# One decoder layer on one core: plain fp32 products, rotation tables on VectorE, and idle ticks in the state-space pipeline

## Chip, cores and metric

The kernel runs on 1 core of one Trainium2 chip. The metric is the device time of one execution in microseconds (us). Runs of a few executions each give a median, and one further execution is taken apart by the hardware profiler.

## What is computed

The reference is one decoder layer that mixes a state-space model (SSM) with sliding-window attention, for a prompt of 2048 tokens and for 8 single sample tokens with stored state, all in fp32. The part that the change touches is the SSM: 64 groups of 16 channels, each with a complex state of 64 numbers.

```python
def ssm_segment(u, hr, hi, ar, ai, bbr, bbi, c_re, c_im):
    xr = jnp.einsum('btgc,gpc->btgp', u, bbr)
    xi = jnp.einsum('btgc,gpc->btgp', u, bbi)
    ...
    _, _, sr, si = lax.associative_scan(
        complex_combine, (jnp.broadcast_to(ar, shp), jnp.broadcast_to(ai, shp), xr, xi), axis=1)
    y = (jnp.einsum('btgp,gcp->btgc', sr, c_re.astype(jnp.float32))
         - jnp.einsum('btgp,gcp->btgc', si, c_im.astype(jnp.float32)))
    return y, sr[:, -1], si[:, -1]
```

Around it stand the projection of the modulated input by `w_in`, the attention, a gated product with `w_glu`, two branch products, the product with `w_out` and a layer norm.

## The kernel before

All large products (line 78, in `chunk_k`) run on TensorE (PE) with operands of type float32r. Each fp32 operand is split into hi and lo, hi on ScalarE (ACT) and the rest on VectorE (DVE), and three products are summed. A job is one block of 128 weight columns against five chunks of tokens (512, 512, 512, 256 and 264), each over 8 slices of 128 features, so 8 x 3 products a chunk.

The program runs in phases. Phase 1 makes the first projections and the SSM's parameters (`ssm_prep`), which are packed into one table a group, `packD`. **Phase 2** (`phase2`) runs 20 jobs of the projection with the SSM woven in: after slices 2, 5 and 7 of every chunk one *tick* of the SSM pipeline is issued, so there are 300 ticks. Phase 3 weaves the attention into more jobs, phases 4 and 5 do the rest.

The SSM works on 32 pairs of groups (`ssm_pairs`). `pipeline` starts a new pair every 9 ticks and gives a pair one stage a tick:

- `load`: the pair's parameters `pk` and inputs `u` come in by DMA, issued by SyncE (SP).
- `b_mat`: DVE makes `bt` in five operations (lines 722 and 724). `rot_tables` makes the rotation tables of the first group.
- `c_mat`: PE transposes `bt` (L752), ACT and DVE split the result `bl` and ACT and GpSimd (POOL) split `u`. DVE makes `ce` in five operations (L759, L761), then come the second group's rotation tables.
- `t_mat`: PE multiplies `pk` by `ce` (L771), ACT copies the result to `kt` (L776), DVE adds a diagonal (L779), SP writes `kt` to DRAM (`tD`) and reads it back shifted as `tt` (L785).
- `x_in`: PE makes `xp` from `bl` and `u`; ACT and DVE split `tt` and `ce`; DVE rotates `xp` into the rotating frame (L798 to L803).
- `scan`: two scans on DVE (L808), four operations that rotate back into `S` (L814 to L817), and a split of `S`.
- an empty stage, then `y_out`: PE makes `yp` from `tt`, `u`, `ce`, `S`; ACT applies gelu (L829), SP stores.

`rot_tables` runs on POOL (lines 744 to 746): six operations of 128 x 256 a group, twelve a pair. The helper `passes` (L703) does three float32r products for one fp32 product, the helper `split` does a copy on ACT (L696) and a subtraction (L697):

```python
for i, (a, b) in enumerate(((wh, xh), (wh, xl), (wl, xh))):
    nc.tensor.matmul(ps, a[:, g], b[:, g, xs], start=first and i == 0, stop=last and i == 2)
```

The scratch tile of `rot_tables` and the tile `kt` share one buffer (tag `tm`, one copy). Each engine executes its own queue in order. That order is set when the program is built, by a scheduler that goes by the priority of the program order and by its own estimate of when operands are ready; so instructions of one pair stand between those of its neighbours.

Of the kernel before, what the change touches and what calls it, by code (L numbers as in the profile page):

```python
# [19 lines left out]
T = 2048  # L20
# [3 lines left out]
G = 64  # L24
# [4 lines left out]
PK = 180  # L29
oBB, oBBs, oW, oWs, oPR, oPI, oRR, oRI, oC1, oS1, oC2, oS2, oR8, oHO, oAH = 0, 16, 32, 48, 64, 73, 82, 90, 98, 114, 130, 146, 162, 164, 172  # L30
# [9 lines left out]
class Trunk:  # L40
# [8 lines left out]
    def split_w(self, parts, st=None):  # L49
        """parts: (dram AP [n, ...], tile slice function)"""  # L50
# [29 lines left out]
    def products(self, jobs, X, nxt=None, tick=None, first=ORD):  # L80
        """jobs: (weight parts, evac(c, ps), begin, end); the next weights are split while a job runs"""
# [26 lines left out]
    def phase_in(self):  # L108
# [32 lines left out]
        with ExitStack() as pes:  # L141
# [36 lines left out]
            def ada(k):  # L178
                """shift and 1 + scale of features 128 k .., by feature"""
# [118 lines left out]
    def ssm_prep(self):  # L298
# [4 lines left out]
        def small(name):  # L303
            return p.tile([128, G], F32, name=name)

        def signed(name, t):
            s = small(name)
# [60 lines left out]
        crs, cis = signed("crs", cr), signed("cis", ci)  # L368
# [6 lines left out]
        for i in range(3):  # L375
            n = (small(f"ec{i}"), small(f"es{i}"))
            self._cmul(v, n, e, e, t1, t2)
            e = n
        e8 = e
        for i in range(4):  # L380
            tg = (f"ec{i % 2}", f"es{i % 2}") if i < 3 else ("fc", "fs")
            n = (small(tg[0]), small(tg[1]))
# [14 lines left out]
        # sample state: h_old and a * h_old  # L397
# [41 lines left out]
        for qd in range(4):  # L439
# [36 lines left out]
            # e^{i n th8}: n = 1..16, and n = 0, 16, .., 240  # L476
            for oC, oS, e, first in ((oC1, oS1, e8, 1), (oC2, oS2, e128, 0)):
# [29 lines left out]
                v.tensor_scalar(pk[0:64, :, oS:oS + 16], pk[0:64, :, oS:oS + 16], -1.0, None, op0=OP.mult)  # L507
                yield
# [162 lines left out]
    def pipeline(units, stages, ii):  # L671
        """at tick t every unit u runs stage t - ii * u, older units first"""
# [9 lines left out]
    def ssm_pairs(self, p, pp, ii):  # L682
# [10 lines left out]
        def split(name, x, eng, bufs=1):  # L693
            hi = p.tile(list(x.shape), F32R, name=name + "h", bufs=bufs)
            lo = p.tile(list(x.shape), F32R, name=name + "l", bufs=bufs)
            nc.scalar.copy(hi, x)  # L696
            eng.tensor_tensor(lo, x, hi, op=OP.subtract)  # L697
            return hi, lo

        def passes(ps, w, x, g, xs, first, last):  # L700
            (wh, wl), (xh, xl) = w, x
            for i, (a, b) in enumerate(((wh, xh), (wh, xl), (wl, xh))):
                nc.tensor.matmul(ps, a[:, g], b[:, g, xs], start=first and i == 0, stop=last and i == 2)  # L703

        def load(s):
# [6 lines left out]
            s["u"] = p.tile([128, 2, 272], F32, name="u", bufs=1)  # L712
# [14 lines left out]
        def rot_tables(s, g):  # L727
            pk = s["pk"]
            if g == 0:
                s["cs"] = p.tile([128, 2, 256], F32, name="cs")  # L730
                s["sn"] = p.tile([128, 2, 256], F32, name="sn")
            tm = p.tile([128, 256], F32, name="tm", bufs=1)
            tv = tm.rearrange("p (a b) -> p a b", a=16)
# [71 lines left out]
        def scan(s):  # L805
# [14 lines left out]
            s["S"] = split("S", S[:, :, 0:264], v)  # L820
# [585 lines left out]
```

## Time and profile before

| what | value |
| --- | --- |
| median of 3 runs | 2398.24 us (2396.42 to 2400.52) |
| span of the profiled execution | 2395.4 us |
| PE busy | 2284.5 us (95%) |
| DVE busy | 1479.4 us (62%) |
| ACT busy | 810.6 us (34%) |
| POOL busy | 678.4 us (28%) |
| DMA, mean over the span | 132 GB/s |

Of the profiled execution the span from the first to the last instruction is what is recorded; the median of the runs is 2.8 us above it. "Busy" counts the time in which an engine has at least one instruction in work; for PE the ends of the products are modelled, so a short stall can hide in it. The share of an engine over the whole span is an average over phases: in the 40 slices of the profile page DVE is at 8 or 9 tenths in slices 7 to 15 (360 to 900 us), at 1 to 2 tenths just before, and lower after.

### The profile page before, as it was taken

The numbers are of one execution on the slowest core, as the hardware profiler recorded it, in microseconds if no ns is written. First come the engines' busy times: TensorE is split into PE (matmuls) and PEld (weight loads), VectorE is DVE, ScalarE is ACT, GpSimd is POOL, SyncE is SP. The second block draws the span as 40 slices with busy tenths as digits, with TensorE's granted clock in tenths as the row PEclk, the third lists the DMA queues.
The fourth block names the chain that finished last, engine by engine and source line by source line (L and its number), as shares of the span: only waits on it lengthen the run. The fifth ranks groups of instructions, "written<-read, shape, count | busy, mean of one in ns | idle before, by whom it ended". The sixth has DMA issues, their size and how long they took to land. (4 is left out here: it accounts for less than half of the span.)

```text
span 2395.4 us, 36160 instructions
## 1 busy us (share of the span) xinstructions
PE 2284.5 (95%) x13011; PEld 1916.6 (80%) x13011; DVE 1479.4 (62%) x3032; ACT 810.6 (34%) x1764; POOL 678.4 (28%) x828
## 2 busy tenths in 40 slices
PE   7999998999999999899999999999999999999998
PEld 5888886777778778777878888887877888888886
DVE  4895129998999996137786666516435214223887
ACT  3411113333222222136675655536223213212100
POOL 1100027666777764000100000012443000222232
PEclk9999999999999999899999999999999999999999
DMA  9453623333343343733334333257535646767431
GB/s 284 101 149 126 197 66 104 102 102 105 99 110 103 104 110 91 143 113 115 101 111 137 103 95 113 82 139 174 153 102 179 199 123 184 218 196 219 156 117 69
DMA packets 388755, 317.03 MB, mean 132 GB/s; under 512 B 90582, under 2 KB 332654, under 8 KB 386991
## 3 DMA queue, kind: packets, MB, share of 16 engines
q1 hardware_dynamic: 388576, 314.73, 45.9%
q8 instruction: 102, 1.67, 0.3%
q14 instruction: 77, 0.63, 0.1%
HBM read 194.75 MB, written 122.11 MB: 132 GB/s over the span
## 5 line engine op out<-in xcount | busy, mean ns | idle before, releaser
L78 PE MATMUL acc<-hh,whi 128*128 128x512 f32 (+2 forms) x2000 | 705.7, 353 | 11.3 <-ACT zr L580 10.5
L78 PE MATMUL acc<-hl,whi 128*128 128x512 f32 (+2 forms) x2000 | 703.9, 352 | 0.0
L78 PE MATMUL acc<-hh,wlo 128*128 128x512 f32 (+2 forms) x2000 | 701.8, 351 | 0.0
L78 PEld LDWEIGHTS acc<-hh,whi 128*128 128x128 f32 x2000 | 379.5, 190 | 63.0 <-ACT zr L580 10.9
L78 PEld LDWEIGHTS acc<-hh,wlo 128*128 128x128 f32 x2000 | 379.8, 190 | 51.8 <-issue 6.7
L78 PEld LDWEIGHTS acc<-hl,whi 128*128 128x128 f32 x2000 | 380.4, 190 | 50.2 <-issue 7.2
L78 PE MATMUL acc<-xh,whi 128*128 128x512 f32 (+2 forms) x960 | 337.3, 352 | 16.6 <-ACT sg L1200 13.9
L78 PE MATMUL acc<-xl,whi 128*128 128x512 f32 (+2 forms) x960 | 336.4, 350 | 1.3 <-DVE xl L1148 1.2
L78 PE MATMUL acc<-xh,wlo 128*128 128x512 f32 (+2 forms) x960 | 335.1, 349 | 0.0
L78 PEld LDWEIGHTS acc<-xh,whi 128*128 128x128 f32 x960 | 182.7, 190 | 44.2 <-ACT sg L1200 17.4
L78 PEld LDWEIGHTS acc<-xl,whi 128*128 128x128 f32 x960 | 182.7, 190 | 26.0 <-DVE xl L1148 3.4
L1078 POOL TENSOR_TENSOR o<-o,z 128x512 f32<-128x512 f32 x32 | 42.6, 1330 | 565.7 <-ACT o L1077 517.7
L78 PEld LDWEIGHTS acc<-xh,wlo 128*128 128x128 f32 x960 | 182.3, 190 | 23.1
L1148 DVE TENSOR_TENSOR xl<-xst,xh 128x1024 fp32r<-128x1024 f32 (+2 forms) x84 | 104.8, 1265 | 78.1 <-ACT xh L1147 77.0
L59 DVE TENSOR_TENSOR wlo<-wst,whi 128x1024 fp32r<-128x1024 f32 x74 | 97.5, 1318 | 86.4 <-ACT whi L58 85.6
L1045 DVE SCALAR_TENSOR_TENSOR t<-ps,bias 128x512 f32<-128x512 f32 (+1 forms) x128 | 82.6, 670 | 98.6 <-PE ps L1043 96.3
L882 ACT ACTIVATE t<-t,nm 128x256 f32<-128x256 f32 (+1 forms) x256 | 125.5, 493 | 46.0 <-DVE es L879 29.9
L1235 POOL TENSOR_TENSOR sg<-sg,zs 128x512 f32<-128x512 f32 (+2 forms) x40 | 48.7, 1219 | 314.0 <-DMA xst<-ysD 190.5
L745 POOL TENSOR_TENSOR tm<-pk 128x256 f32<-128x256 f32 x128 | 106.8, 834 | 65.2 <-DMA tD<-kt 59.0
L1147 ACT CAST xh<-xst 128x1024 fp32r<-128x1024 f32 (+2 forms) x84 | 86.0, 1044 | 102.2 <-DMA xst<-mD 33.9
L58 ACT CAST whi<-wst 128x1024 fp32r<-128x1024 f32 x74 | 77.6, 1049 | 102.9 <-PE acc L78 95.1
L580 ACT COPY zr<-acc 128x512 f32<-128x512 f32 (+2 forms) x120 | 59.9, 500 | 137.0 <-PE acc L78 58.1
(372 smaller groups left out, 3935.2 us busy)
## 6 DMA issues: line engine op xcount, KB each, us to landing
wst<-in_w_in SPq DMA_DIRECT2D x50, 512.0 KB
uD<-u SPq DMA_DIRECT2D x8, 1088.0 KB
u<-uD SPq DMA_DIRECT2D x32, 272.0 KB
yD<-y SPq DMA_DIRECT2D x64, 132.0 KB
x<-in_x_prompt SPq DMA_DIRECT2D x16, 512.0 KB
wa<-in_w_ada SPq DMA_DIRECT2D x16, 512.0 KB
qf<-qD SPq DMA_DIRECT2D x32, 256.0 KB
z<-zaP SPq DMA_DIRECT2D x32, 256.0 KB
```

The costliest lines, as they stand in the source:

```text
L58: nc.scalar.copy(hi, st)
L59: nc.vector.tensor_tensor(lo, st, hi, op=OP.subtract)
L78: self.nc.tensor.matmul(ps[:, :n], w[:, k, :], x[:, k, :], start=(k == 0 and i == 0), stop=(k == KT - 1 and i == 2))
L580: nc.scalar.copy(z[:, :n], ps[:, :n])
L745: gq.tensor_tensor(tv, up(x2), lo(y2), op=OP.mult)
L882: nc.scalar.activation(t1[:, h, kw], t1[:, h, kw], AF.Exp, bias=nm[:, h:h + 1], accum_out=den[:, h:h + 1])
L1045: v.scalar_tensor_tensor(t1[:, 2 * g:2 * g + 2, kw], ps[:, :, kw], 0.125, s["bias"][:, hd, b0:b0 + kw.stop], op0=OP.mult, op1=OP.add)
L1078: nc.gpsimd.tensor_tensor(o4, o4, s["z4"], op=OP.mult)
L1147: nc.scalar.copy(xv(hi[:, k - 1:k + 1]), sv(st))
L1148: nc.vector.tensor_tensor(xv(lo[:, k - 1:k + 1]), sv(st), xv(hi[:, k - 1:k + 1]), op=OP.subtract)
L1235: gq.tensor_tensor(t[:, :n], t[:, :n], pa[:, :n], op=OP.add)
```

## The change

- **Products.** The SSM's products take the fp32 operands as they are, one instruction where three stood. The splits of `bl`, `u`, `tt`, `ce` and `S` go, with their ten float32r tiles.
- **Rotation tables.** `rot_tables` moves from POOL to DVE. Cosine and sine of a group stand in one tile and are made by three operations of 128 x 512 instead of six of 128 x 256. This needs a table `-S` of 16 more numbers a group in `packD` (196 instead of 180), made by one more DVE operation for each quarter of the groups in `ssm_prep`.
- **Idle ticks and buffers.** Empty stages are put after `load`, after `x_in` and after `scan`: 12 stages instead of 8, so the last pair ends at tick 291 instead of 287. `u`, `ce`, `tt` and `S` get two buffers instead of one. The tile `tm` is twice as large, still one copy, and still shared with `kt`.
- In `ssm_prep` some small tiles share buffers by tag.

```diff
-PK = 180
+PK = 196
...
             for oC, oS, e, first in ((oC1, oS1, e8, 1), (oC2, oS2, e128, 0)):
...
+                if not first:
+                    v.tensor_scalar(pk[:, :, oN2:oN2 + 16], S, -1.0, None, op0=OP.mult)
...
-            s["u"] = p.tile([128, 2, 272], F32, name="u", bufs=1)
+            s["u"] = p.tile([128, 2, 272], F32, name="u")
...
-            for out, (x1, y1), (x2, y2), op in ((s["cs"], (oC2, oC1), (oS2, oS1), OP.subtract),
-                                                (s["sn"], (oS2, oC1), (oC2, oS1), OP.add)):
-                ov = out[:, g].rearrange("p (a b) -> p a b", a=16)
-                gq.tensor_tensor(ov, up(x1), lo(y1), op=OP.mult)
-                gq.tensor_tensor(tv, up(x2), lo(y2), op=OP.mult)
-                gq.tensor_tensor(ov, ov, tv, op=op)
+            ov = s["rot"][:, :, g].rearrange("p e (a b) -> p e a b", a=16)
+            v.tensor_tensor(ov, up(oC2), lo(oC1), op=OP.mult)
+            v.tensor_tensor(tm.rearrange("p e (a b) -> p e a b", a=16), up(oN2), lo(oS1), op=OP.mult)
+            v.tensor_tensor(s["rot"][:, :, g], s["rot"][:, :, g], tm, op=OP.add)
...
-            s["bl"] = split("bl", ps, v)
-            s["us"] = split("u", s["u"], gq, 2)
-            ce = s["ce"] = p.tile([128, 2, 9, 16], F32, name="ce", bufs=1)
+            s["bl"] = p.tile([128, 2, 128], F32, name="bl", bufs=1)
+            nc.scalar.copy(s["bl"], ps)
+            ce = s["ce"] = p.tile([128, 2, 9, 16], F32, name="ce")
...
-                passes(xp[:, g, :264], s["bl"], s["us"], g, slice(8, 272), True, True)
-            s["tts"] = split("tt", s["tt"], v)
-            s["ces"] = split("ce", s["ce"][:, :, 1:9].rearrange("p g j c -> p g (j c)"), v)
+                nc.tensor.matmul(xp[:, g, :264], s["bl"][:, g], s["u"][:, g, 8:272], start=True, stop=True)
...
-            s["S"] = split("S", S[:, :, 0:264], v)
...
-                passes(yp[:, g, :264], s["tts"], s["us"], g, slice(0, 264), True, False)
-                passes(yp[:, g, :264], s["ces"], s["S"], g, slice(0, 264), False, True)
+                nc.tensor.matmul(yp[:, g, :264], s["tt"][:, g], s["u"][:, g, 0:264], start=True, stop=False)
+                nc.tensor.matmul(yp[:, g, :264], s["ce"][:, g, 1:9].rearrange("p j c -> p (j c)"), s["Sf"][:, g, 0:264],
+                                 start=False, stop=True)
...
-        stages = [load, b_mat, c_mat, t_mat, x_in, scan, lambda s: None, y_out]
+        stages = [load, gap, b_mat, c_mat, t_mat, x_in, gap, scan, gap, gap, gap, y_out]
```

How the built order moves is seen at three places. First DVE, a stretch of phase 2 from the making of `ce` to the scans; before, the subtractions of the splits (L697) stand among them:

```order
L759 TENSOR_TENSOR tmp<-pk 128x144 x2
L697 TENSOR_TENSOR bll<-tr,blh 128x256
L697 TENSOR_TENSOR cel<-ce,ceh 128x256
L759 TENSOR_TENSOR ce<-pk 128x144 x2
L779 TENSOR_TENSOR kt<-dg,tr 16x16 x2
L798 TENSOR_TENSOR t_7336<-xp,cs 128x512
L799 TENSOR_TENSOR S<-xp,sn 64x2x256
L800 TENSOR_TENSOR S<-xp,sn 64x2x256
L802 TENSOR_TENSOR hnew<-pk,xp 128x16
L761 TENSOR_TENSOR ce<-ce,tmp 128x288
L803 TENSOR_TENSOR t_7336<-t_7336,S 128x512
```

and now:

```order
L750 TENSOR_TENSOR ce<-ce,tmp 128x288
L768 TENSOR_TENSOR kt<-dg,tr 16x16 x2
L785 TENSOR_TENSOR t_6819<-xp,rot 128x512
L786 TENSOR_TENSOR S<-xp,rot 64x2x256
L787 TENSOR_TENSOR S<-xp,rot 64x2x256
L789 TENSOR_TENSOR hnew<-pk,xp 128x16
L734 TENSOR_TENSOR tm<-pk 128x512
L790 TENSOR_TENSOR t_6819<-t_6819,S 128x512
L735 TENSOR_TENSOR rot<-rot,tm 128x2x256
L795 SCALAR_TENSOR_TENSOR t_6819<-pk,t_6819 128x256 x2
L734 TENSOR_TENSOR tm<-pk 128x512
```

The splits are gone, the whole of `ce` now stands right ahead of `kt`, and the first write of `tm` by the next pair's table (L734) stands five instructions after `kt` (L768), whose buffer it takes over.

Second PE, the end of a pair's `yp`, its successor's `t_mat` and `xp`; before (L703 is one float32r pass):

```order
L703 MATMUL yp<-Sl,ceh 128x264
L703 MATMUL yp<-Sh,cel 128x264
L771 MATMUL tr<-ce,pk 32x128 x2
L703 MATMUL xp<-uh,blh 128x264
L703 MATMUL xp<-ul,blh 128x264
L703 MATMUL xp<-uh,bll 128x264
L703 MATMUL xp<-uh,blh 128x264
```

and now:

```order
L813 MATMUL yp<-S,ce 128x264
L812 MATMUL yp<-u,tt 128x264
L813 MATMUL yp<-S,ce 128x264
L78 MATMUL acc<-hl_833,whi 128x512
L78 MATMUL acc<-hh_832,wlo 128x512
L760 MATMUL tr<-ce,pk 32x128 x2
L780 MATMUL xp<-u,bl 128x264 x2
```

The order of the pieces is the same; where three or nine passes stood, one or three fp32 products stand. In both orders the products of L78 from the first `xp` to the last are the same in number.

Third SP, the DMA issues of one pair, now (before, the order is the same in kind, with L783, L785, L711 in place of L772, L774, L701):

```order
L701 DMA pk<-packD_77 128x392
L558 DMA qD_95<-kq 128x512
L55 DMA wst<-in_w_in 128x8x128
L703 DMA u<-uD_84 128x2x272
L818 DMA yD_91<-y 8x16x264 x2
L558 DMA qD_95<-kq 128x512
L772 DMA tD_3585<-kt 16x8x128 x2
L774 DMA tt<-tD_3585 128x2x128
```

Loads and stores of a pair wait in one queue with the stores of the projection; none of them moved to another queue.

## Rows read from the trace of the kernel before

**Rows 1.** Busy time by stretch, two stretches of phase 2: PE, PEld, DVE, ACT, POOL.

```profile
core 0: us, PE busy (x) PEld busy (x) DVE busy (x) ACT busy (x) POOL busy (x), PEclk, DMA share, GB/s
340.00:905.00 565.00, 512.16 (x2864) 432.00 (x2864) 522.12 (x867) 172.62 (x336) 393.28 (x555) 0.98 0.37 103
350.00:900.00 550.00, 499.24 (x2796) 421.45 (x2795) 507.74 (x845) 168.78 (x328) 379.62 (x537) 0.98 0.37 105
```

**Rows 2.** One line's instructions (L703): ns min/median/max, first and last start in us.

```profile
L703 PE MATMUL xp<-uh,blh x64: 280/284/587, 345.2 to 929.1; 128*128 128x264 f32 x64
```

**Rows 3.** Groups of PE, 340 to 905 us: count | busy us, mean ns | idle before.

```profile
L703 PE MATMUL yp<-uh,ttl 128*128 128x264 f32 x59 | 19.4, 328 | 10.5 <-DVE ttl L697 10.0
L703 PE MATMUL yp<-Sh,ceh 128*128 128x264 f32 x58 | 19.0, 328 | 16.3 <-ACT Sh L696 15.9
```

**Rows 4.** Waits in 340 to 905 us: us in total, times, longest.

```profile
ACT tth L696 <- DMA tt<-tD: 115.6, 27, 7.1
POOL tm L745 <- DMA tD<-kt: 56.5, 25, 5.0
...
DVE tmp L722 <- DMA pk<-packD: 2.8, 3, 1.0
```

**Rows 5.** Groups of DVE, 340 to 905 us (columns as in rows 3).

```profile
L722 DVE TENSOR_TENSOR tmp<-pk 128x128 f32<-128x128 f32 x62 | 37.4, 636 | 3.0 <-DMA pk<-packD 2.8
...
L817 DVE TENSOR_TENSOR S<-t,S 128x512 f32<-128x512 f32 x30 | 33.3, 1109 | 0.0
...
L798 DVE TENSOR_TENSOR t<-xp,cs 128x512 f32<-128x512 f32 x30 | 20.6, 687 | 6.6 <-PE xp L703 6.1
...
L761 DVE TENSOR_TENSOR ce<-ce,tmp 128x288 f32<-128x288 f32 x31 | 16.0, 517 | 0.1
```

**Rows 6.** DVE instructions by line, whole span (columns as in rows 2).

```profile
L722 DVE TENSOR_TENSOR tmp<-pk x64: 277/709/1446, 337.8 to 904.2; 128x128 f32<-128x128 f32 x64
...
L816 DVE TENSOR_TENSOR t<-t,cs x32: 678/1108/1226, 361.7 to 937.8; 128x512 f32<-128x512 f32 x32
...
L808 DVE TENSOR_TENSOR_SCAN t<-pk,t x64: 658/692/1221, 359.0 to 934.3; 128x256 f32<-128x256 f32 x64
...
L759 DVE TENSOR_TENSOR tmp<-pk x64: 293/307/1471, 340.8 to 910.5; 128x144 f32<-128x144 f32 x64
```

**Rows 7.** Groups of POOL, 340 to 905 us (columns as in rows 3).

```profile
L745 POOL TENSOR_TENSOR tm<-pk 128x256 f32<-128x256 f32 x123 | 102.4, 832 | 62.5 <-DMA tD<-kt 56.5 <-ACT zr L580 1.6
...
L774 POOL TENSOR_TENSOR dg<-ident,dT 16x16 f32<-16x16 f32 x60 | 18.3, 306 | 49.2 <-DVE kt L779 47.0
L819 POOL COPY sfin<-S 128x2 f32<-128x2 f32 x29 | 11.3, 391 | 1.2 <-DVE S L817 1.2
L812 POOL COPY S<-pk 128x16 f32<-128x16 f32 x29 | 8.1, 279 | 11.7 <-DVE Sl L697 10.3 <-DVE kt L779 1.3
```

**Rows 8.** Timeline of PE: start us, duration us; float32r products in a row.

```profile
897.07 0.39 PE L78 MATMUL acc<-hh,whi 128*128 128x512 f32 x1
...
901.15 0.39 PE L78 MATMUL acc<-hh,whi 128*128 128x512 f32 x1
...
908.97 0.28 PE L703 MATMUL yp<-uh,tth 128*128 128x264 f32 x1
...
909.71 0.28 PE L78 MATMUL acc<-hh,wlo 128*128 128x256 f32 x1
```

**Rows 9.** Timeline of PE in phase 3: four plain fp32 products and what follows.

```profile
982.72 1.06 PE L936 MATMUL po<-kts,qm 128*128 128x129 f32 x8
983.61 0.27 PE L930 MATMUL pt<-ident,kc 128*128 128x128 f32 x1
```

**Rows 10.** Timeline of DVE, one pair's `kt` and the operation after `x_in`'s first four.

```profile
616.27 0.35 DVE L779 TENSOR_TENSOR kt<-dg,tr 16x16 f32<-16x16 f32 x2 [1.10 <-ACT kt L776]
...
618.87 1.24 DVE L697 TENSOR_TENSOR cel<-ce,ceh 128x256 fp32r<-128x256 f32 x1
```

**Rows 11.** Timeline of SP, the same pair: the stores of `kt`, then the load that waits for them.

```profile
616.46 0.79 SPq L783 DMA_DIRECT2D tD<-kt  x2
619.24 0.38 SPq L785 DMA_DIRECT2D tt<-tD  x1
```

More of the change, by code (lines that the diff above doesn't have):

```diff
@@ L28 @@
 U0, ZS0, Q0, K0, V0, ZA0, GS0, GA0 = 0, 1024, 2048, 3072, 3328, 3584, 4608, 5632
-PK = 180
-oBB, oBBs, oW, oWs, oPR, oPI, oRR, oRI, oC1, oS1, oC2, oS2, oR8, oHO, oAH = 0, 16, 32, 48, 64, 73, 82, 90, 98, 114, 130, 146, 162, 164, 172
+PK = 196
+oBB, oBBs, oW, oWs, oPR, oPI, oRR, oRI, oC1, oS1, oN2, oC2, oS2, oR8, oHO, oAH = 0, 16, 32, 48, 64, 73, 82, 90, 98, 114, 130, 146, 162, 178, 180, 188
 def _bucket(dist):
@@ L301, in ssm_prep, with small, signed @@
         p, pq, pp = self.prp, self.prp, self.sps
[L303 to L307, printed above, removed]
+        def small(name, tag=None):
+            return p.tile([128, G], F32, name=name, tag=tag or name)
+        def signed(name, t, tag):
+            s = small(name, tag)
             v.tensor_scalar(s[0:64], t[0:64], -1.0, None, op0=OP.mult)
@@ L367, in ssm_prep @@
         v.tensor_tensor(ci, t1, den, op=OP.mult)
-        crs, cis = signed("crs", cr), signed("cis", ci)
+        crs, cis = signed("crs", cr, "dt"), signed("cis", ci, "lr")
         yield
@@ L375, in ssm_prep @@
         for i in range(3):
-            n = (small(f"ec{i}"), small(f"es{i}"))
+            n = (small(f"ec{i}", ("e_x", "hf", "nr")[i]), small(f"es{i}", ("e_r", "th", "den")[i]))
             self._cmul(v, n, e, e, t1, t2)
@@ L380, in ssm_prep @@
         for i in range(4):
-            tg = (f"ec{i % 2}", f"es{i % 2}") if i < 3 else ("fc", "fs")
-            n = (small(tg[0]), small(tg[1]))
+            tg = (("e_x", "e_r"), ("hf", "th"), ("e_x", "e_r"), ("mag", "li"))[i]
+            n = (small(f"fc{i}", tg[0]), small(f"fs{i}", tg[1]))
             self._cmul(v, n, e, e, t1, t2)
@@ L691, in ssm_pairs @@
             nc.sync.dma_start(tD[i][:, 256:368], zt)
[L693 to L703, printed above, removed]
         def load(s):
@@ L729, in rot_tables, with up @@
             if g == 0:
[L730 to L733, printed above, removed]
-            def lo(o):
-                return pk[:, g, None, o:o + 16].to_broadcast([128, 16, 16])
-            def up(o):
-                return pk[:, g, o:o + 16, None].to_broadcast([128, 16, 16])
-            for out, (x1, y1), (x2, y2), op in ((s["cs"], (oC2, oC1), (oS2, oS1), OP.subtract),
-                                                (s["sn"], (oS2, oC1), (oC2, oS1), OP.add)):
-                ov = out[:, g].rearrange("p (a b) -> p a b", a=16)
-                gq.tensor_tensor(ov, up(x1), lo(y1), op=OP.mult)
-                gq.tensor_tensor(tv, up(x2), lo(y2), op=OP.mult)
-                gq.tensor_tensor(ov, ov, tv, op=op)
+                s["rot"] = p.tile([128, 2, 2, 256], F32, name="rot")
+                s["cs"], s["sn"] = s["rot"][:, 0], s["rot"][:, 1]
+            tm = p.tile([128, 2, 256], F32, name="tm", bufs=1)
+            B = [128, 2, 16, 16]
+            def up(o):
+                return pk[:, g, o:o + 32].rearrange("p (e a) -> p e a", e=2)[:, :, :, None].to_broadcast(B)
+            def lo(o):
+                return pk[:, g, None, None, o:o + 16].to_broadcast(B)
+            ov = s["rot"][:, :, g].rearrange("p e (a b) -> p e a b", a=16)
+            v.tensor_tensor(ov, up(oC2), lo(oC1), op=OP.mult)
+            v.tensor_tensor(tm.rearrange("p e (a b) -> p e a b", a=16), up(oN2), lo(oS1), op=OP.mult)
+            v.tensor_tensor(s["rot"][:, :, g], s["rot"][:, :, g], tm, op=OP.add)
         def c_mat(s):
@@ L783, in t_mat @@
                 nc.sync.dma_start(dst, kt[32 * g:32 * g + 16, None].to_broadcast([16, 8, 128]))
-            s["tt"] = p.tile([128, 2, 128], F32, name="tt", bufs=1)
+            s["tt"] = p.tile([128, 2, 128], F32, name="tt")
             nc.sync.dma_start(s["tt"], td[:, :512].rearrange("p (g x) -> p g x", x=256)[:, :, 0:128])
@@ L790, in x_in @@
             for g in range(2):
-                passes(xp[:, g, :264], s["bl"], s["us"], g, slice(8, 272), True, True)
-            s["tts"] = split("tt", s["tt"], v)
-            s["ces"] = split("ce", s["ce"][:, :, 1:9].rearrange("p g j c -> p g (j c)"), v)
+                nc.tensor.matmul(xp[:, g, :264], s["bl"][:, g], s["u"][:, g, 8:272], start=True, stop=True)
             t1 = s["t1"] = p.tile([128, 2, 256], F32, name="t1", bufs=1)
-            s["Sf"] = p.tile([128, 2, 265], F32, name="S", bufs=1)
+            s["Sf"] = p.tile([128, 2, 265], F32, name="S")
             t2 = s["Sf"][:, :, 9:265]
@@ L825, in y_out @@
             for g in range(2):
[L826 to L828 removed]
+                nc.tensor.matmul(yp[:, g, :264], s["tt"][:, g], s["u"][:, g, 0:264], start=True, stop=False)
+                nc.tensor.matmul(yp[:, g, :264], s["ce"][:, g, 1:9].rearrange("p j c -> p (j c)"), s["Sf"][:, g, 0:264],
+                                 start=False, stop=True)
+            y = p.tile([128, 2, 264], F32, name="y", bufs=1)
             nc.scalar.activation(y, yp[:, :, :264], AF.Gelu_apprx_tanh)
@@ L831, in y_out, with gap @@
                 nc.sync.dma_start(self.yD[m][(gl + g) * 16:(gl + g + 1) * 16].rearrange("c j n -> j c n"), y[:, g])
-        stages = [load, b_mat, c_mat, t_mat, x_in, scan, lambda s: None, y_out]
+        def gap(s):
+            pass
+        stages = [load, gap, b_mat, c_mat, t_mat, x_in, gap, scan, gap, gap, gap, y_out]
         return self.pipeline([{"pr": i} for i in range(32)], stages, ii)
```

1 line of the change is left out of this document (removed).

## Prediction

> **What bounds the kernel now.** PE is busy for 95% of the span, so the first idea is that only PE work counts. I looked for the phase in which that is not so. The row of slices has DVE at 8 or 9 tenths from 360 to 900 us, where the SSM is woven into the projection. The table by stretch says it in numbers [rows 1]: from 350 to 900 us DVE is busy for 507.74 of 550 us (92%), POOL for 379.62, and PE for 499.24, so PE has gaps of at least 9%. I then read which work sets the pace. The first `xp` product of the 32 pairs starts at 345.2 us, the last at 929.1 [rows 2]: 584 us for 31 pairs, **18.83 us a pair**.
>
> What PE would need for that is counted from its timeline [rows 8]. From 897.07 to 901.15 us eighteen 512-column float32r products start, one every 0.227 us; from 908.97 to 909.71 six of 264 columns, one every 0.123. (The printed durations, 0.39 and 0.28, overlap; starts are what to read.) Nine ticks are three chunks of 24 products, 72 products; over the five chunk widths their mean is (3 x 0.227 + 2 x 0.123) / 5 = 0.185 us, so 13.3 us. Eighteen SSM passes make 2.2 us, transposes and `t_mat` about 0.5: 16.0 us. PE thus stalls for some 2.8 us a pair. It waits in `yp` for the splits of `tt` and of `S` [rows 3], that is for DVE and ACT. ACT itself stands before the split of `tt`, waiting for a DMA, 115.6 us in all [rows 4]. But DVE, with 92%, has only 18.83 x 0.08 = 1.4 us a pair in which it does not work, so it is the engine to follow.
>
> Part of that work is waiting in disguise. The same operation takes very different times: 277 ns at least and 709 in the median for 128 elements, 678 and 1108 for 512 [rows 6]. Those that read PSUM do not stretch: L798 has a mean of 687 ns [rows 5]. The stretched ones read two operands in SBUF while POOL makes its tables. Mean less shortest, times the count, gives 62 x (636 - 277) = 22.3 us for the first row of [rows 5]; over all sixteen such groups of that view (the first and the last are shown) it is 155 us, against 393 us of POOL work [rows 1]: 0.39 us of DVE time lost for each us of POOL.
>
> **The change, part by part.** All prices are for one pair, in us.
>
> *Products.* Eighteen float32r passes go, six fp32 products come. Phase 3 has plain fp32 of 129 columns: eight records from 982.72 to 983.61, two to a product [rows 9], 0.111 each; for 264 columns 0.227, or 0.454 a product. So 2.2 us become 2.7: **PE gets 0.5 us more work**, 16.5 in all. That is no gain; it costs nothing only as long as DVE sets the pace.
>
> *Splits.* Three subtractions of 256 elements, one of 528, and POOL's of `u` go, with five copies on ACT. In `yp`, PE then waits for `tt` and `S` alone, and ACT's queue is no longer held by the wait for the DMA of `tt`.
>
> *Tables.* POOL loses its twelve operations; what stays there is L774 twice, L819 and L812, 2 x 0.306 + 0.391 + 0.279 [rows 7], with a small memset about 1.37 us. DVE gains six operations of 512 elements.
>
> *DVE after.* Alone, by the shortest times [rows 6]: fourteen operations of 512 elements (six of the tables, four in `x_in`, four after the scans) at 0.685 make 9.6; two scans 1.32; four of 128 and four of 144 elements 1.11 and 1.20; the sums for `bt` and `ce`, `kt` and `hnew` 1.3. With 20 weight splits of 1.2 and 30 gates of `z_a` at 0.4 to 0.68 spread over 32 pairs (1.3), this is 15.85. POOL's rest costs 0.39 x 1.37 = 0.5; the bounds are nothing and 1.37. Successive operations overlap: in 340 to 905 us DVE's groups add up to 553 us where it was busy for 522 [rows 1], so the 16.4 count as **15.4**. Before, 0.92 x 18.83 = 17.4.
>
> *DVE's waits after.* In the new order `ce` stands just ahead of `kt`, and `t_mat` on PE and the copy on ACT lie between them; then `x_in` needs `xp`, which PE makes right behind `t_mat`. The pair shown waited 1.10 for `kt` [rows 10]; with 0.9 of fp32 products for `xp` behind it I take 1.4. New is a wait for DMA: L734 overwrites the buffer of `kt` and must wait until `kt` has been stored. In the pair shown the stores are issued at 616.46 and the load behind them starts at 619.24, so they take up to 2.8 [rows 11]; `x_in`'s first four operations end at 618.87, 2.2 after `kt` [rows 10]. That leaves 0.4; POOL's own waits for it had a mean of 56.5 / 25 = 2.3 [rows 4]. I take 0.6, near the pair shown, because DVE no longer runs ahead as POOL did. The next pair's parameters can only be loaded after the scans, and L712 follows sooner than before: 0.2, with 1.0, the longest such wait now [rows 4], as bound. Behind each of these stands all of DVE's queue, and PE behind that at `t_mat`. Sum: 2.2. The idle ticks keep `yp` away from these waits: on PE about 13 us of other work lie between `xp` and the `yp` that needs its scan, on DVE 12.
>
> *Sum.* 15.4 + 2.2 = 17.6 for DVE, 16.5 for PE: DVE still sets the pace, but nearer to PE; I take **17.5**. 31 x (18.83 - 17.5) = 41 us. The first `xp` stands behind some 1.4 us more of other products, and the tail is about as long as before: 39 us. The added negation in `ssm_prep` and the larger table cost nothing: they lie in phase 1, where DVE is at 1 or 2 tenths in the last slices. Phases 3 to 5 keep their work. The sum is against the profiled execution (2395.4 to 2356); the median of the runs stands 2.8 above that, so 2398.2 becomes **2359**.
>
> A rule of the Trainium skill speaks against part of this: "SBUF — State Buffer", section "Who interferes with whom", calls the pair of ports that DVE and GpSimd share an exclusive lock, where the loser is blocked for a whole instruction. By that the POOL work that stays would cost its full time. The rows show 0.39 us lost a us, an average over operations that use the pair and others that do not.
>
> **The rivals.**
>
> *PE becomes the bound.* If DVE's waits hide under the idle ticks, a pair takes PE's 16.5. For: the waits are small and single; the order leaves PE work between all handovers except `t_mat` to `xp`. Against: `t_mat` needs `ce`, which DVE makes 3.5 us after `S` in its queue, while PE gets from `yp` to `t_mat` in some 2. 31 x 2.33 = 72 us, 2326. Chance 0.17.
>
> *What is left on POOL blocks in full.* Each of its short operations reads SBUF and stands in the middle of DVE's chain (`kt`'s diagonal, the copies around the scan). At 1.37 instead of 0.5 a pair, 18.4: 13 us less, 2385. The rule of the Trainium skill gives this case. For: the stretch of 128-element operations from 277 to 709 ns is more than their own length. Against: they stretched beside operations of 0.8 us back to back, not beside 0.3 us. Chance 0.08.
>
> *No change.* The two DMA waits and the handover take the 1.3 us that the tables' move frees: 2398, or the change does not free DVE because the stretching was something other than POOL. Chance 0.05.
>
> *Slower.* DVE's queue now stands behind the stores of `kt`. If SP, which issues them in one queue with the stores of the projection, is late, DVE waits 2.3 as POOL did, 1.7 more than I took, and 0.8 more for `pk`: 20.0 a pair, 36 us more, 2434. It decides from 1.33 us of further waits a pair on. For: SP's queue is as full as before. Against: in the pair shown the issue came at once. Chance 0.12.
>
> **How the numbers follow.** My forecast, DVE at 17.0 to 18.0 a pair, has 0.58. Without the chances of "same" and "slower", 0.58 + 0.17 + 0.08 = 0.83 is for faster by over 0.2% (about what a measurement here can tell from no change), 0.05 for same, 0.12 for slower. The range goes from the PE bound at 2325 to just short of no change, 2396; beyond it lie the slower case and about half of "same". The forecast's own part is 2343 to 2375.
>
> **What would show it.** From the first `xp` to the last 542 us instead of 584. DVE's operations with two operands in SBUF near their shortest times, 0.69 us for 512 elements. POOL nearly idle there. DVE busy for about 88%. Waits of DVE for `kt`'s stores of about 0.6 us a pair at L734, and of PE at L760 for `ce`; none of ACT for `tt`, few of PE in `yp`. It is wrong if DVE's durations stay stretched with POOL idle, if L734 waits 2 us, or if fp32 products of 264 columns start more than 0.25 us apart a record.

## The result, and the profile after

The kernel before took 2397.45 us (median of 4 runs, 2396.42 to 2400.52), the changed one **2340.75 us** (4 runs, 2339.37 to 2345.57): 0.9764 of the time, 95% interval 0.975 to 0.9778, 57 us less. The forecast was 2359 with a range of 2325 to 2396; the sign and the range hold, the size was 18 us short.

The profiled execution has a span of 2339.3 us. First the busy time by stretch, the same two stretches as [rows 1], columns as there:

```profile
core 0: us, PE busy (x) PEld busy (x) DVE busy (x) ACT busy (x) POOL busy (x), PEclk, DMA share, GB/s
340.00:905.00 565.00, 558.24 (x2986) 468.71 (x2985) 463.75 (x973) 130.94 (x235) 65.83 (x167) 1.00 0.40 113
350.00:900.00 550.00, 543.24 (x2900) 456.00 (x2899) 453.32 (x947) 128.73 (x230) 65.18 (x163) 1.00 0.40 113
```

PE is busy for 543.24 of 550 us, 99%, where it was 499.24; DVE fell from 92% to 82%, POOL from 379.62 us to 65.18. The roles are exchanged: **PE now sets the pace, and DVE waits.** The clock that TensorE was granted (PEclk, as a share of 2.4 GHz) is 1.00 in both stretches, where it was 0.98: before, it fell to its lower level of 1.2 GHz for short whiles, so that 440 to 450 us, for one, show 0.83. In 550 us that is up to 550 x 0.02 = 11 us of PE's time, an estimate; no run tells what part of the gain it is. The instructions of the `xp` product, to set against [rows 2], give the pace (two records to a product, so 128 of them):

```profile
L780 PE MATMUL xp<-u,bl x128: 383/387/491, 346.2 to 873.7; 128*128 128x264 f32 x128
```

From the first to the last pass 527.5 us instead of 584: **17.02 us a pair instead of 18.83**, 56 us in all, which is the whole gain. Between the first and the last `xp` stand 2215 products of the projection in both kernels, so the two figures may be compared. The groups of PE from 350 to 900 us (columns as in [rows 3]) show what is left of its waits:

```profile
L78 PE MATMUL acc<-hh,whi 128*128 128x512 f32 (+2 forms) x776 | 282.8, 364 | 0.0
...
L813 PE MATMUL yp<-S,ce 128*128 128x264 f32 x128 | 39.5, 391 | 5.5 <-DVE S L804 5.5
L812 PE MATMUL yp<-u,tt 128*128 128x264 f32 x128 | 39.2, 388 | 1.3 <-DMA tt<-tD 1.3
L780 PE MATMUL xp<-u,bl 128*128 128x264 f32 x124 | 35.6, 410 | 0.0
L760 PE MATMUL tr<-ce,pk 128*32 128x128 f32 x124 | 13.2, 285 | 0.0
```

Only `yp` waits at all, 6.8 us in 550. L760, the product of `t_mat`, waits for nothing. Next the groups of DVE from 340 to 905 us, against [rows 5, 6], four of the rows that were stretched there and one of the new ones:

```profile
L734 DVE TENSOR_TENSOR tm<-pk 128x512 f32<-128x512 f32 x63 | 43.1, 684 | 29.3 <-DMA tD<-kt 28.8
L795 DVE TENSOR_TENSOR_SCAN t<-pk,t 128x256 f32<-128x256 f32 x64 | 40.6, 676 | 0.1
...
L804 DVE TENSOR_TENSOR S<-t,S 128x512 f32<-128x512 f32 x32 | 22.1, 690 | 0.6
...
L712 DVE TENSOR_TENSOR tmp<-pk 128x128 f32<-128x128 f32 x62 | 15.3, 286 | 1.7 <-DMA pk<-packD 1.3
...
L750 DVE TENSOR_TENSOR ce<-ce,tmp 128x288 f32<-128x288 f32 x32 | 14.6, 457 | 0.9
```

L804 means 690 ns where the same operation, L817, meant 1109; L712 means 286 where L722 meant 636. All stand near the shortest times that such operations had before. DVE's waits from 350 to 900 us, against [rows 4] (us in total, times, longest):

```profile
DVE tm L734 <- DMA tD<-kt: 28.8, 25, 2.6
...
DVE kt L768 <- ACT kt L765: 13.1, 14, 2.6
DVE ce L748 <- PE yp L813: 9.7, 8, 1.8
...
DVE t L785 <- PE xp L780: 5.9, 14, 0.8
```

These four come to 57.5 us, 1.8 a pair (550 us are 32.3 pairs); with the waits left out here DVE is idle for 2.4 a pair (71.55 of 500 us from 350 to 850). And what stays on POOL, against [rows 7]:

```profile
L806 POOL COPY sfin<-S 128x2 f32<-128x2 f32 x32 | 36.3, 1134 | 298.6 <-DVE S L804 296.8 <-PE tr L741 1.8
L763 POOL TENSOR_TENSOR dg<-ident,dT 16x16 f32<-16x16 f32 x62 | 15.5, 249 | 123.3 <-DVE kt L768 121.0
L799 POOL COPY S<-pk 128x16 f32<-128x16 f32 x31 | 7.9, 254 | 19.4 <-issue 12.8 <-PE yp L813 2.8 <-POOL sfin L806 1.5
```

The copy `sfin`, 391 ns on average before, now takes 1134: beside DVE it seems to be POOL that is held up, and no other engine waits for this copy.

### The profile page after: what moved, and what is told of

Read it like the earlier page. It is cut to its first block, busy times and chain, and to the rows that moved or that the text cites. A ratio compares the mean times of both kernels' runs of the same rounds, so it can differ in the third digit from the quotient of the medians.

```text
span 2339.3 us, 35133 instructions
## 1 busy us (share of the span) xinstructions
PE 2274.6 (97%) x12819; PEld 1903.5 (81%) x12819; DVE 1393.7 (60%) x3100; ACT 755.1 (32%) x1636; POOL 329.1 (14%) x412
## 5 line engine op out<-in xcount | busy, mean ns | idle before, releaser
L78 PE MATMUL acc<-hh,whi 128*128 128x512 f32 (+2 forms) x2000 | 714.0, 358 | 11.2 <-ACT zr L582 10.7
L78 PE MATMUL acc<-hl,whi 128*128 128x512 f32 (+2 forms) x2000 | 706.7, 353 | 0.0
L78 PE MATMUL acc<-hh,wlo 128*128 128x512 f32 (+2 forms) x2000 | 703.2, 352 | 0.0
L78 PEld LDWEIGHTS acc<-hh,whi 128*128 128x128 f32 x2000 | 378.3, 189 | 64.8 <-ACT zr L582 11.1
L78 PEld LDWEIGHTS acc<-hl,whi 128*128 128x128 f32 x2000 | 378.6, 189 | 53.1 <-issue 7.6
L78 PEld LDWEIGHTS acc<-hh,wlo 128*128 128x128 f32 x2000 | 378.1, 189 | 53.1 <-issue 6.9
L78 PE MATMUL acc<-xh,whi 128*128 128x512 f32 (+2 forms) x960 | 336.5, 351 | 15.1 <-ACT sg L1190 13.3
L78 PE MATMUL acc<-xl,whi 128*128 128x512 f32 (+2 forms) x960 | 335.5, 349 | 3.0 <-DVE xl L1138 2.9
L78 PE MATMUL acc<-xh,wlo 128*128 128x512 f32 (+2 forms) x960 | 333.7, 348 | 0.0
L78 PEld LDWEIGHTS acc<-xh,whi 128*128 128x128 f32 x960 | 181.5, 189 | 43.5 <-ACT sg L1190 17.8
L78 PEld LDWEIGHTS acc<-xl,whi 128*128 128x128 f32 x960 | 181.7, 189 | 27.7 <-DVE xl L1138 5.4
L78 PEld LDWEIGHTS acc<-xh,wlo 128*128 128x128 f32 x960 | 181.5, 189 | 23.0
L1330 PE MATMUL po<-wol,xh 128*128 128x512 f32 (+1 forms) x272 | 102.8, 378 | 0.8 <-DVE wol L1253 0.8
L1330 PE MATMUL po<-woh,xh 128*128 128x512 f32 (+1 forms) x272 | 102.8, 378 | 0.1
```

Source lines behind the costliest of these rows:

```text
L78: self.nc.tensor.matmul(ps[:, :n], w[:, k, :], x[:, k, :], start=(k == 0 and i == 0), stop=(k == KT - 1 and i == 2))
L1330: nc.tensor.matmul(ps[:, :w], X[a][:, k, ts], Wo[h * w // 512][b][:, k, ws], start=(i == 0), stop=(i == 23))
```

## The experiments

Each run is given as a ratio to the kernel before, measured on the same chip. The table has busy time in the stretch from 350 to 850 us and the pace, that is from the first to the last record of `xp`, over 31 pairs (for the kernel before 18.84, since the last of the three passes is taken). In two kernels the scheduler spread the pairs over many more products of the projection than 2215, and there the pace can't be compared; in the others it is 2209 to 2221. Line numbers in the rows are those of each kernel.

| kernel | ratio, 95% interval | PE | DVE | POOL | us a pair |
|---|---|---|---|---|---|
| before | 1 | 453.57 | 461.24 | 343.86 | 18.84 |
| changed | 0.9764 [0.975, 0.9778] | 493.24 | 428.45 | 61.77 | 17.02 |
| tables on POOL | 1.0051 [1.0034, 1.0069] | 452.44 | 420.07 | 243.95 | 19.23 |
| tables alone | 0.9764 [0.974, 0.9789] | 482.92 | 484.14 | 137.48 | 17.11 |
| idle ticks alone | 0.9933 [0.9914, 0.9951] | 463.25 | 457.14 | 355.16 | 18.43 |
| fp32 alone | 0.9923 [0.9906, 0.9941] | 477.81 | 390.39 | 303.60 | (2459 products) |
| POOL tables, unread | 1.0152 [1.0135, 1.0169] | 440.19 | 475.07 | 292.84 | 20.01 |
| POOL memsets | 0.9752 [0.9737, 0.9766] | 494.53 | 430.32 | 340.24 | 16.98 |
| without `tt` x `u` | 0.9617 [0.9603, 0.9631] | 496.51 | 448.81 | 68.70 | 16.05 |
| without idle ticks | 0.9739 [0.9725, 0.9754] | 496.44 | 432.18 | 55.78 | 16.84 |
| changed, again | 0.975 [0.9736, 0.9764] | 492.42 | 427.39 | 64.15 | 17.06 |
| more on DVE | 0.9744 [0.973, 0.9757] | 496.15 | 463.59 | 75.34 | 16.93 |
| no ticks, one buffer each | 0.9924 [0.9911, 0.9938] | 477.16 | 358.65 | 36.21 | (2747 products) |
| part of the products split | 0.9695 [0.9682, 0.9708] | 495.88 | 464.43 | 115.33 | 16.65 |

### The parts of the change, one at a time

*Tables on POOL*: all of the change, with the three new table operations on GpSimd.

```diff
-            v.tensor_tensor(ov, up(oC2), lo(oC1), op=OP.mult)
+            gq.tensor_tensor(ov, up(oC2), lo(oC1), op=OP.mult)
...
```

> The changed kernel with its three table operations a group back on POOL (same shapes, 128 x 512). If PE sets the pace after the change, DVE has room: it loses 4.1 us of table work a pair and gets back 0.39 us for each us of POOL's tables (some 9 us), about the same sum, so the time stays within 6 us of 2341. If the place of the tables is what gained, DVE's operations stretch again and the time goes back by 25 us or more, to 2366 or above.

It took 2407.47 us, slower than before. All that the rest of the change brings is lost when the tables stay on POOL. Its groups show both costs at once, long operations on POOL that wait, and stretched ones on DVE (350 to 850 us; first three groups of POOL, then one of DVE):

```profile
L735 POOL TENSOR_TENSOR rot<-rot,tm 128x512 f32<-128x512 f32 x52 | 82.4, 1584 | 3.7
L734 POOL TENSOR_TENSOR tm<-pk 128x512 f32<-128x512 f32 x52 | 70.3, 1352 | 60.9 <-DMA tD<-kt 55.6 <-ACT kq L556 3.7
L733 POOL TENSOR_TENSOR rot<-pk 128x512 f32<-128x512 f32 x52 | 56.9, 1114 | 22.9 <-DVE t L803 22.9
```

```profile
L804 DVE TENSOR_TENSOR S<-t,S 128x512 f32<-128x512 f32 x26 | 35.9, 1382 | 0.0
```

Since DVE was busy only 84% here, the run can't say which of the two costs decided.

*Tables alone*: the kernel before, with only the tables moved to VectorE in the new form (and the negated row that they read).

```diff
...
-                gq.tensor_tensor(ov, up(x1), lo(y1), op=OP.mult)
-                gq.tensor_tensor(tv, up(x2), lo(y2), op=OP.mult)
-                gq.tensor_tensor(ov, ov, tv, op=op)
...
+            v.tensor_tensor(ov, up(oC2), lo(oC1), op=OP.mult)
+            v.tensor_tensor(tm.rearrange("p e (a b) -> p e a b", a=16), up(oN2), lo(oS1), op=OP.mult)
+            v.tensor_tensor(s["rot"][:, :, g], s["rot"][:, :, g], tm, op=OP.add)
```

> The kernel before with the tables alone moved to DVE in the new form (splits, stages and single buffers as before). DVE gives back about 4.0 us of stretch a pair (0.39 x 10.3 us of POOL tables) and takes on 4.1 us of tables: if DVE's work sets the pace there, no more than 10 us off 2397. If the stretch by POOL alone was the loss, 30 us faster or more.

It took 2338.82 us: **this part by itself brings all of the gain**, against what I expected. DVE got six operations more, 4.1 us, and yet its busy time a pair fell from 17.4 to 16.6 (484.14 of 500 at 17.11): 4.9 us of stretching went. One of its groups from 350 to 850 us, which stood at 1109 ns before (L817):

```profile
L818 DVE TENSOR_TENSOR S<-t,S 128x512 f32<-128x512 f32 x29 | 19.8, 682 | 0.0
```

That is 0.8 of the 1.7 us a pair that the run gained. The other 0.9 is DVE's idle time, 0.5 a pair instead of 1.5; what ended those waits is not shown. DVE (97%) and PE (97%) are both near their limit here.

*Idle ticks alone* and *fp32 alone*, again on the kernel before:

```diff
-        stages = [load, b_mat, c_mat, t_mat, x_in, scan, lambda s: None, y_out]
+        stages = [load, gap, b_mat, c_mat, t_mat, x_in, gap, scan, gap, gap, gap, y_out]
```

> The kernel before with the new stages (idle ticks) alone. If DVE's work sets the pace, at most its waits of 1.4 us a pair can go: 2360 to 2398, likely within 15 us of 2397. If PE's waits for late operands (splits of S and tt) are what is lost, the idle ticks give 30 us or more by themselves: 2367 or less.

```diff
-                passes(xp[:, g, :264], s["bl"], s["us"], g, slice(8, 272), True, True)
+                nc.tensor.matmul(xp[:, g, :264], s["bl"][:, g], s["u"][:, g, 8:272], start=True, stop=True)
...
-            s["S"] = split("S", S[:, :, 0:264], v)
```

> Plain fp32 products alone: no splits, but tables on POOL in the old form, old stages, single buffers. DVE loses 1.9 us of splits and some 0.5 us of stretch a pair, PE gains 0.5 us of work: if DVE sets the pace before, 2.4 us a pair less until PE bounds at 16.5 to 17: 2340 to 2370. If the depth of the pipeline is what gains, within 10 us of 2397.

2379.08 and 2376.88 us, against 2393.91 for the kernel before in the same set: 15 and 17 us. The first was within what I expected, the second brought less. So the parts don't add up: 55 (the tables), 15 and 17 alone, 57 together, and 14 lost when all but the tables' move is made. The tables and the products lighten the same engine, DVE, and once it is lighter than PE, more of it is worth nothing. Why the rest of the change loses 14 us where the tables stay on POOL is open, and so is what the ticks alone gain by.

### What the tables cost on POOL

If the gain came from DVE's stretched operations, then GpSimd work that nobody needs must bring the loss back. If it came from tables that arrived late, it must not. The second run below keeps GpSimd as busy, but without reading.

```diff
...
+            for (x1, y1), (x2, y2), op in (((oC2, oC1), (oS2, oS1), OP.subtract), ((oS2, oC1), (oC2, oS1), OP.add)):
+                gq.tensor_tensor(oz, up1(x1), lo1(y1), op=OP.mult)
+                gq.tensor_tensor(tv, up1(x2), lo1(y2), op=OP.mult)
+                gq.tensor_tensor(oz, oz, tv, op=op)
```

> The changed kernel, with the tables on VectorE as there; besides, GpSimd makes the twelve 128x256 table operations of before once more for every pair, into tiles that nobody reads. PE and VectorE thus get no work and, by their data, no wait. If moving the tables gained because VectorE's operations stretch while GpSimd reads two operands in SBUF (0.39 us lost for each us of GpSimd work, counted on the trace of before), some 10.5 us of GpSimd work a pair stretch VectorE from 14.6 us busy a pair by 4.1, to 18.7 and more: VectorE sets the pace again, 31 x (18.7 - 17.0) = 53 us, 2390 to 2400. If it gained because VectorE and PE waited for late tables (their latency on GpSimd), nothing waits here for them, and the time stays at 2341 within 8 us.

```diff
+            oq = p.tile([128, 512], F32, name="oq", bufs=1)
+            for i in range(9):
+                gq.memset(oq, 0.0)
```

> As the run before, but what GpSimd does besides is eighteen memsets of 128x512 a pair, some 9.6 us by the 311 ns of the 128x256 memset in the trace of before: it is as busy, writes SBUF and reads nothing. If any GpSimd work stretches VectorE, the time is as in the run before, 2380 to 2400. If only operations that read two operands in SBUF do, it stays at 2341 within 8 us. By the Trainium skill, "SBUF — State Buffer", section "Who interferes with whom", it is the second.

The first took 2432.44 us, 92 more than the changed kernel, 20.01 us a pair; the second 2335.87, no more than the changed one. The first is 32 us above what I expected at most: VectorE's busy time came as forecast (19.0 a pair, below), but it was idle for another 1.0, which I had left out; TensorE's granted clock was 0.95 in that stretch. **It is contention for operands in SBUF, not lateness.** Two groups of DVE in the first run, one that also stretched before and one that reads PSUM:

```profile
L819 DVE TENSOR_TENSOR S<-t,S 128x512 f32<-128x512 f32 x25 | 27.0, 1080 | 0.4
...
L800 DVE TENSOR_TENSOR t<-xp,rot 128x512 f32<-128x512 f32 x25 | 17.3, 690 | 1.1 <-PE xp L795 0.4
```

1080 ns beside 690, as [rows 5] had 1109 beside 687. In the second run the memsets keep POOL busy for 289.9 us in 500, by the group of POOL from 350 to 850 us:

```profile
L734 POOL MEMSET oq<- 128x512 f32 x551 | 289.9, 526 | 28.9
```

DVE's operation of the same kind stays short there, by its group in the same stretch:

```profile
L807 DVE TENSOR_TENSOR S<-t,S 128x512 f32<-128x512 f32 x30 | 20.6, 688 | 0.5
```

How the two engines meet is seen on the timelines of the first run. First POOL (start us, duration us):

```profile
614.21 1.05 POOL L746 TENSOR_TENSOR oq<-oq,tq 128x256 f32<-128x256 f32 x1
615.34 0.95 POOL L744 TENSOR_TENSOR oq<-pk 128x256 f32<-128x256 f32 x1
616.25 1.07 POOL L745 TENSOR_TENSOR tq<-pk 128x256 f32<-128x256 f32 x1
```

And DVE beside it, two operations in one row:

```profile
614.60 2.24 DVE L748 TENSOR_TENSOR rot<-pk 128x512 f32<-128x512 f32 x2
```

Two operations that take 685 ns each in the changed kernel fill 2.24 us. The first starts while POOL's of 614.21 runs, which ends at 615.26; the pair ends at 616.84, 0.55 after POOL's second, which ends at 616.29. The ends alternate, POOL's and DVE's, as they would if the two took turns, one instruction at a time. The Trainium skill, "SBUF — State Buffer", section "Who interferes with whom", has a rule for this: a VectorE instruction with two SBUF inputs contends with a GpSimd instruction that reads SBUF, not with one that only writes it, and what they contend for is an exclusive lock. Both halves of the first part agree with these runs: 1080 ns beside reads, 688 beside memsets.

The size: DVE was busy for 475.07 / 500 x 20.01 = 19.0 us a pair instead of 428.45 / 500 x 17.02 = 14.6. The added operations of POOL were busy for 266.3 us in 500 (L746 98.4, L744 85.9, L745 82.0), 10.7 a pair. **4.43 / 10.66 = 0.42 us of DVE lost for each us of POOL**, where the prediction had 0.39 from [rows 1, 5].

### Which engine sets the pace after

Two runs, one that takes work from PE alone and one that gives DVE more:

```diff
-                nc.tensor.matmul(yp[:, g, :264], s["tt"][:, g], s["u"][:, g, 0:264], start=True, stop=False)
...
-                                 start=False, stop=True)
+                                 start=True, stop=True)
```

> The changed kernel without the products of tt and u: y lacks the part that comes from the tokens of its own chunk. It takes four fp32 records of 0.224 us, 0.9 us a pair, from PE, and nothing from VectorE. If PE sets the pace (99% busy from 350 to 850 us), 31 x 0.9 = 28 us go, down to about 2313, or less if VectorE, at 14.6 busy and 2 waiting, becomes the bound on the way: 2313 to 2328. If VectorE's queue sets the pace, as I predicted, the time stays within 4 us of 2341.

```diff
             v.tensor_tensor(t2, t1, t2, op=OP.subtract)
+            v.tensor_tensor(t1, t1, cs, op=OP.mult)
+            v.tensor_tensor(t1, t1, cs, op=OP.mult)
```

> The changed kernel with two more products of 128x512 on VectorE for each pair, on a buffer that is no longer needed: 2 x 0.686 = 1.37 us a pair more for VectorE, nothing for PE. If VectorE's queue sets the pace, as I predicted, 31 x 1.37 = 43 us more. If PE does, VectorE takes it out of the 2.4 us a pair in which it now waits (14.6 us busy of 17.02): 0 to 12 us more, the upper end where its waits don't move.

Without the product the time was 2303.7 us, 37 less than the changed kernel in the first set (33 less than in the last): 16.05 us a pair, so 0.97 less for four records that were priced at 0.9. It went 9 us beyond the lower end of what I expected; phase 2 accounts for 31.6 us (its end, marked by the first plain fp32 product of phase 3, moved from 915.0 to 883.4 us), and the rest lies in later phases, whose code is the same. With 1.37 us a pair more on DVE the time was 2335.09, next to 2336.98 for the changed kernel in the same set, and the intervals overlap. Both say PE. The waits show where DVE took the time from: at L734, 14.4 us in 500 instead of 27.9, and at `kt` 4.4 instead of 12.1.

### Idle ticks and buffers

```diff
-        stages = [load, gap, b_mat, c_mat, t_mat, x_in, gap, scan, gap, gap, gap, y_out]
+        stages = [load, b_mat, c_mat, t_mat, x_in, scan, gap, y_out]
```

> The changed kernel with the stages of before: no idle ticks, so scan follows x_in, and y_out comes two stages behind the scan. The idle ticks alone were worth 15 us on the kernel before. If they keep PE from waiting in yp for the scan, they are worth more where PE is the bound: PE then waits in yp some 0.5 to 1 us a pair, 2355 to 2375. If with VectorE freed the waits are short without them, 2341 to 2348.

The same, with one buffer each for `u`, `ce`, `tt` and `S`:

```diff
...
-            ce = s["ce"] = p.tile([128, 2, 9, 16], F32, name="ce")
+            ce = s["ce"] = p.tile([128, 2, 9, 16], F32, name="ce", bufs=1)
...
-            s["Sf"] = p.tile([128, 2, 265], F32, name="S")
+            s["Sf"] = p.tile([128, 2, 265], F32, name="S", bufs=1)
```

> The changed kernel without the idle ticks and with one buffer each for u, ce, tt and S: of the change there remain the fp32 products and the tables on VectorE. Without the ticks and with the buffers it took 0.9739 of before. If the buffers matter now that ce and S are read by the products themselves (no split copies behind them), VectorE stands at ce and at S until yp has read those of the pair before, 1 to 2 us a pair: 2360 to 2390. If yp runs before VectorE gets there, 2330 to 2340, and that whole part of the change is worth nothing.

> The changed kernel once more, so that the others of this set stand beside it on one chip: 0.976 of before, within 0.002.

Without the ticks: 2332.25 us, below both ranges that I gave, and 16.84 a pair instead of 17.02 and 17.06. So beside the other two parts the ticks bring nothing and seem to cost some 4 to 6 us in phase 2 (it ended at 910.9 us instead of 915.0 and 916.5); as whole times, 0.9739 against 0.9764 and 0.975, the intervals overlap. **The double buffers are what matters of that part**: without them too it was 2378.81, 46 us more. They matter beside the fp32 products: the run with the tables alone had one buffer each and was as fast as the changed kernel. The waits of DVE, 350 to 850 us:

```profile
DVE ce L748 <- PE yp L813: 52.0, 23, 4.8
DVE kt L768 <- ACT kt L765: 35.4, 20, 3.5
```

The first is what I expected: `ce` is now read by `yp` itself, so with one buffer DVE stands at `ce` until the pair before is through. The second bears on my prediction's error. The order of the DVE queue, here with the numbers of the buffers, first of this run:

```
L748 TENSOR_TENSOR ce_6434<-pk_6398 128x144 x2
L750 TENSOR_TENSOR ce_6434<-ce_6434,tmp_6435 128x288
...
L768 TENSOR_TENSOR kt_6466<-dg_6465,tr_6464 16x16 x2
...
L789 TENSOR_TENSOR hnew_3582<-pk_6398,xp_6487 128x16
```

And of the changed kernel:

```
L748 TENSOR_TENSOR ce_6612<-pk_6554 128x144 x2
L750 TENSOR_TENSOR ce_6612<-ce_6612,tmp_6613 128x288
L768 TENSOR_TENSOR kt_6475<-dg_6474,tr_6473 16x16 x2
...
L789 TENSOR_TENSOR hnew_3582<-pk_6389,xp_6493 128x16
```

With one buffer, the `ce` ahead of `kt` is made from `pk_6398`, and `hnew` behind it reads `pk_6398` too: it is the same pair, so `t_mat` and the copy on ACT have only the five operations between them in DVE's queue to hide behind, and `kt` waits 35.4 us in some 24 pairs, 1.5 each. With two buffers the `ce` ahead of `kt` is made from `pk_6554`, while `hnew` reads `pk_6389`: it is the next pair's, and the `ce` that `t_mat` needs was made a pair earlier. The wait at `kt` did not go altogether: it is 13.1 us in 14 waits in the changed kernel, 0.4 a pair, and 32.0 us in 500 in the run with the tables on POOL, which has two buffers as well. What holds `t_mat` up there was not tested.

### A version that beats both

PE is the bound, and fp32 costs it 0.5 us a pair more than the split products. So, without the ticks, I gave the products with `u` back their three float32r passes and left only `ce` with `S` in fp32, whose split was the largest on DVE.

```diff
...
-                nc.tensor.matmul(xp[:, g, :264], s["bl"][:, g], s["u"][:, g, 8:272], start=True, stop=True)
+                passes(xp[:, g, :264], s["bl"], s["us"], g, slice(8, 272), True)
+            s["tts"] = split("tt", s["tt"], v)
...
-                nc.tensor.matmul(yp[:, g, :264], s["tt"][:, g], s["u"][:, g, 0:264], start=True, stop=False)
+                passes(yp[:, g, :264], s["tts"], s["us"], g, slice(0, 264), False)
```

> A try at less PE work: without the idle ticks, and the products with u (xp, and tt with u in yp) as three float32r passes again, with the splits of bl and tt on VectorE and of u on GpSimd; only ce with S stays fp32. PE: twelve passes of 0.123 for eight fp32 records of 0.224, 1.48 for 1.79, 0.31 less a pair; VectorE two subtractions of 256 elements, about 0.8 more, and some 0.5 of stretching by GpSimd's 1.4 us. If PE sets the pace and the order holds, 31 x 0.31 = 10 us less than without the idle ticks alone (0.9739 of before): 0.970. If VectorE, at 15.9 busy and 1.5 to 2 of waits, comes ahead of PE, 0.976 to 0.985.

2322.73 us (4 runs), 0.9695 of before and 14 us below the changed kernel in the same set; the intervals, 0.9682 to 0.9708 and 0.9736 to 0.9764, are apart. The pace went from 16.84 to 16.65, 0.19 of the 0.31 that I counted, but with nine more products of the projection between the first and the last `xp`; by the end of phase 2, which holds the same ones, the gain is 8.9 us (910.9 to 902.0), near the 10 that I expected. PE stays the bound, with DVE at 93%.

## Why the prediction was right, and where it was not

- **What bounded the kernel before** was read rightly: DVE, by operations stretched beside POOL. Moving the tables alone brings it all, about half of it by DVE's busy time and half by its waits, and bringing back unread POOL work loses it again, at 0.42 us a us instead of 0.39.
- **Products.** A record of 264 columns was priced at 0.227 us from [rows 9]. In the changed kernel the timeline of PE shows blocks like this one:

```profile
618.70 0.40 PE L78 MATMUL acc<-hh,wlo 128*128 128x512 f32 x1
619.02 0.41 PE L760 MATMUL tr<-ce,pk 128*32 128x128 f32 x4
619.37 1.16 PE L780 MATMUL xp<-u,bl 128*128 128x264 f32 x4
620.17 0.59 PE L78 MATMUL acc<-hh,whi 128*128 128x512 f32 x1
620.59 0.39 PE L78 MATMUL acc<-hl,whi 128*128 128x512 f32 x1
```

  The last three of those four records start 0.22 us apart, so the price was right. What was short is the rest of PE's sum: 16.5, and 17.0 came. The stretch from 618.70 to 619.37 holds one projection product (0.227) and `t_mat`, which thus takes 0.44; I had 0.5 for it and the transposes of `bt` together, and those come to about 0.2 by the starts around them. The waits in `yp` are 0.2 more. Some 0.2 stay open.
- **DVE's own work** was put at 15.4 and came at 14.6. What stays on POOL, which I charged with 0.5, costs DVE nothing that shows, its operations being near their shortest times; it is POOL's copy that got long (1134 ns). So the rival in which that rest blocks DVE in full fell. The other part is the overlap of successive operations, of which I had counted only a part: the 553 us are the groups' busy times, in which operations of one group that overlap count once, while the 15.85 is made of single durations. Those add up to 564 us in 340 to 905 us of before, 1.4 a pair more than the 522 of busy time, and after, in 350 to 850 us, to 471.6 where DVE was busy for 428.45, 1.5 a pair. I took 1.0.
- **DVE's waits** were put at 2.2 and came at 1.8 a pair, but not as I had them: for `kt`'s stores 0.9 instead of 0.6, for `kt` and `xp` together 0.6 instead of 1.4, for `pk` nothing instead of 0.2, and 0.3 for `ce` behind `yp`, which I had not listed. With PE as the bound most of this is slack, as the run with more on DVE showed.
- **The step that failed** is DVE's waits, and in them the handover: "In the new order `ce` stands just ahead of `kt`, and `t_mat` on PE and the copy on ACT lie between them". The order was read without the numbers of the buffers. That `ce` belongs to the next pair; it is the pair's own only with one buffer, where `kt` alone waits 1.5 us. So 0.6 came of the 1.4. How little DVE has to wait is shown by the run with more on DVE: it was busy there for 15.7 us a pair and idle for 1.2 (463.59 of 500 us at 16.93), with PE still setting the pace. Even the 15.4 as forecast would thus have fitted under PE's 17.0, and "15.4 + 2.2 = 17.6 for DVE, 16.5 for PE: DVE still sets the pace" did not come. The two other terms erred the same way, DVE's work by 0.8 too much and PE's by 0.5 too little.
- **Range and luck.** What came is the mechanism of the first rival, which I gave 0.17, with its price 0.5 a pair too low. The time lies in the range because the range was drawn out to that rival's bound; it is 2 us below the forecast's own part (2343 to 2375). The sign rests on the reading of the kernel before, which held; the size was set by another engine than the one that I forecast.
- **The slower rival** decided from 1.33 us of further waits a pair on. L734 waited 0.3 more than I took.
- **Phases 3 to 5** kept their time, as forecast: from the first plain fp32 product of phase 3 (971.6 us before, 915.0 after) to the end 1423.8 and 1424.3 us.

## What to carry to other kernels

Where an engine's operations show twice their shortest time, look for who reads SBUF at the same time before counting instructions: moving work onto the busier engine can leave it with less busy time for each unit of work. Work out the load of every engine after a change, and take the largest; parts that lighten the same engine don't add up, and from where the next engine binds they only cost it. When a program's order is read for who waits for whom, read it with the numbers of the buffers, since a neighbour of the same name may belong to another unit.

## What was not expected of the hardware

- GpSimd at 68% busy with memsets (340.24 of 500 us) cost VectorE nothing that shows: 430.32 us busy against 428.45, and 0.9752 of before against 0.9764 and 0.975.
- Where short GpSimd operations meet a dense VectorE queue, it is GpSimd that loses: a copy of 128x2 took 1134 ns on average, 185 at least. That fits the turns above, seen from the other side; no run tests it.
- One float32r pass of 264 columns takes 0.123 us, one fp32 product of two records 0.447. So three split passes, 0.37, are cheaper on PE than the one fp32 product that replaces them; what the split costs lies on the other engines.
